# RMSNorm with SiLU on one core: all transfers in turns on one queue

## The chip, the core and the metric

The kernel runs on one core of a Trainium2 chip. The core has a matrix engine (PE), a vector engine (DVE), a scalar engine (ACT), GpSimd (POOL) and SyncE (SP), each with an instruction stream of its own that it works through in order. Data move between device memory (HBM) and the core's own memory (SBUF, 128 partitions) by 16 DMA engines, to which instructions on ACT and SP hand transfers; the page calls the queue that ACT feeds q10 and the one that SP feeds q1. The metric is the device time of one execution in microseconds (us). Lower is better.

## The reference

```python
def setup_inputs():
    batch, seq_len, hidden = 8, 1024, 2048
    return {
        "x": np.random.randn(batch, seq_len, hidden).astype(np.float32),
        "gamma": np.random.randn(hidden).astype(np.float32),
        "eps": np.float32(1e-5),
    }

def reference(x, gamma, eps):
    rms = np.sqrt(np.mean(x ** 2, axis=-1, keepdims=True) + eps)
    out = gamma * x / rms
    return (out * (1 / (1 + np.exp(-out)))).astype(np.float32)
```

There are 8192 rows of 2048 float32 values. Each row is divided by its root mean square, multiplied by gamma and passed through SiLU. Input and output are 67.1 MB each.

## The kernel before

The rows are cut into 16 blocks of 512 rows (4 MB). In a block each of the 128 partitions holds four whole rows that are neighbours in memory, so one partition's share is a run of 32 KB. Six tiles `xt` (BUFS = 6) hold blocks in SBUF, and all work is done in place.

For one block: the squares of each row are summed, some rows on ACT (`squares_scalar`, line 65) and the rest on DVE (`squares_vector`, line 73). `share(b)` on line 78 says how many of the four rows ACT takes: one for the even blocks 4 to 12, two otherwise. ACT then takes the root of the four sums (`root`, line 82), DVE inverts it (`invert`, line 87) and multiplies each row by its own factor and by gamma (`multiply`, line 92). ACT applies SiLU to two rows at a time (`silu`, line 98), and the block is stored (line 102). Root and SiLU use different function tables, so ACT loads a table when it goes from one to the other; squares need no load of their own. The last block is multiplied by gamma alone on DVE (line 155), and ACT applies the row factors as the scale of SiLU (line 157).

Loads are issued on ACT's queue (line 54): blocks 0 and 1 first, blocks 2 to 5 after ACT has waited for gamma (line 116), and each later block b+3 after the first square of block b+1 (lines 67 to 69, 129), when the store that frees its tile has landed. Stores are issued on SP's queue, each when its block's SiLU is done.

Gamma comes in first on SP's queue, as one row of 8 KB on one partition (line 110). PE spreads it over all partitions by matrix products with a column of ones (line 113), and DVE copies the result to `g` (line 115).

The order on ACT and DVE is written out by hand (lines 128 to 149). For each block b the loop places the multiply and SiLU of b among the squares and root of b+1: in the middle (b from 3 to 13) the squares and root of b+1 come ahead of multiply and SiLU of b; at the start and the end the multiply comes first, and SiLU stands between the scalar squares and the root.

Of the kernel before, what the change touches and what calls it, by code (L numbers as in the profile page):

```python
# [1 line left out]

# [4 lines left out]

ACT = mybir.ActivationFunctionType
ALU = mybir.AluOpType


@with_exitstack
def kernel(
    ctx: ExitStack,
    tc: tile.TileContext,
    x: bass.AP,
    gamma: bass.AP,
    eps: bass.AP,
    out: bass.AP,
):  # L20

    nc = tc.nc
    P = nc.NUM_PARTITIONS
    f32 = mybir.dt.float32
    x2 = x.flatten_outer_dims()
    o2 = out.flatten_outer_dims()  # L30
    n, d = x2.shape
    J = 4
    BUFS = 6
    nblk = n // (P * J)
    xb = x2.rearrange("(b p j) d -> b p (j d)", p=P, j=J)
    ob = o2.rearrange("(b p j) d -> b p (j d)", p=P, j=J)

    singles = ctx.enter_context(tc.tile_pool(name="singles", bufs=1))
    pool = ctx.enter_context(tc.tile_pool(name="pool", bufs=BUFS))
    small = ctx.enter_context(tc.tile_pool(name="small", bufs=2))  # L40
    psum = ctx.enter_context(tc.tile_pool(name="psum", bufs=1, space=bass.MemoryType.PSUM))

    Q = 4
    w = d // Q
    g = singles.tile([P, d], f32)
    eps_t = singles.tile([P, 1], f32)
    ones = singles.tile([P, P], f32)
    junk_a = psum.tile([P, d], f32, name="junk_a")
    junk_v = psum.tile([P, d], f32, name="junk_v")
    blocks, sss, rmss, rstds = {}, {}, {}, {}  # L50

    def load(b):
        xt = pool.tile([P, J * d], f32, name="xt")
        nc.scalar.dma_start(out=xt, in_=xb[b])  # L54
        blocks[b] = xt

    def row(b, j):
        return blocks[b][:, j * d:(j + 1) * d]

    def squares_scalar(b, loads=()):  # L60


        sss[b] = small.tile([P, J], f32, name="ss")
        for j in range(share(b)):
            nc.scalar.activation(out=junk_a, in_=row(b, j), func=ACT.Square,  # L65
                                 accum_out=sss[b][:, j:j + 1])
            if j == 0:
                for s in loads:
                    load(s)

    def squares_vector(b):
        for j in range(share(b), J):
            nc.vector.tensor_tensor_reduce(  # L73
                out=junk_v, in0=row(b, j), in1=row(b, j), scale=1.0, scalar=0.0,
                op0=ALU.mult, op1=ALU.add, accum_out=sss[b][:, j:j + 1])

    def share(b):
        return 1 if 4 <= b <= 12 and b % 2 == 0 else 2

    def root(b):  # L80
        rms = small.tile([P, J], f32, name="rms")
        nc.scalar.activation(out=rms, in_=sss.pop(b), func=ACT.Sqrt, scale=1.0 / d, bias=eps_t)  # L82
        rmss[b] = rms

    def invert(b):
        rstd = small.tile([P, J], f32, name="rstd")
        nc.vector.reciprocal(out=rstd, in_=rmss.pop(b))  # L87
        rstds[b] = rstd

    def multiply(b):  # L90
        for j in range(J):
            nc.vector.scalar_tensor_tensor(out=row(b, j), in0=row(b, j), scalar=rstds[b][:, j:j + 1],  # L92
                                           in1=g, op0=ALU.mult, op1=ALU.mult)

    def silu(b):
        for h in range(0, J, 2):
            cols = slice(h * d, (h + 2) * d)
            nc.scalar.activation(out=blocks[b][:, cols], in_=blocks[b][:, cols], func=ACT.Silu)  # L98
        store(b)

    def store(b):
        nc.sync.dma_start(out=ob[b], in_=blocks[b])

    with tc.manual_schedule():

        load(0)
        nc.vector.memset(ones, 1.0)  # L107
        nc.vector.memset(eps_t, float(eps))
        nc.scalar.activation(out=junk_a[:, 0:1], in_=ones[:, 0:1], func=ACT.Square)  # L109
        nc.sync.dma_start(out=g[0:1, :], in_=bass.AP(tensor=gamma.tensor, offset=gamma.offset, ap=[[d, 1], [1, d]]))  # L110
        for c in range(Q):
            cols = slice(c * w, (c + 1) * w)
            nc.tensor.matmul(junk_v[:, cols], ones[0:1, :], g[0:1, cols], start=True, stop=True)  # L113
        load(1)
        nc.vector.tensor_copy(out=g, in_=junk_v)  # L115
        nc.scalar.copy(out=junk_a[:, 0:1], in_=junk_v[:, d - 1:d])  # L116
        for b in range(2, BUFS):
            load(b)

        last = nblk - 1
        SOON = 3
        squares_scalar(0)
        squares_vector(0)
        root(0)
        invert(0)
        for b in range(last):
            loads = [b + 3] if BUFS <= b + 3 < nblk else []
            if b < SOON:  # L130
                multiply(b)
                squares_scalar(b + 1, loads)
                silu(b)
                squares_vector(b + 1)
                root(b + 1)
            elif b < last - 1:
                squares_scalar(b + 1, loads)
                squares_vector(b + 1)
                root(b + 1)
                multiply(b)  # L140
                silu(b)
            else:
                multiply(b)
                squares_scalar(b + 1)
                silu(b)
                squares_vector(b + 1)
                root(b + 1)
            if b + 1 < last:
                invert(b + 1)


        for j in range(J):
            if j == J // 2:
                invert(last)
            nc.vector.tensor_mul(out=row(last, j), in0=row(last, j), in1=g)  # L155
        for j in range(J):
            nc.scalar.activation(out=row(last, j), in_=row(last, j), func=ACT.Silu,  # L157
                                 scale=rstds[last][:, j:j + 1])
        store(last)


# [1 line left out]
_INS = ['x', 'gamma', 'eps']  # L163
_OUTS = [((8, 1024, 2048), 'float32')]

_NUMBERS = {'eps': 9.999999747378752e-06}


# [26 lines left out]
```

## Time and profile before

| | |
|---|---|
| time, median of 3 runs | 316.97 us (316.77 to 317.25) |
| span of the profiled execution | 315.1 us |
| DVE busy | 235.3 us (75%) |
| ACT busy | 213.9 us (68%) |
| PE busy | 7.2 us (2%) |
| DMA packets | 4613, 134.24 MB, mean 426 GB/s over the span |
| loads | 16, 4096 KB each, median 38.7 us from issue to landing |
| stores | 16, 4096 KB each, median 29.0 us from issue to landing |
| DVE's longest wait by line | 42.2 us for loads, ahead of line 73 |

The span runs from the first to the last instruction that the profiler recorded; 1.8 us of the runs' median lie around it. Busy time is time in which an engine computes; issuing a transfer is not counted. The profile's parts used below are the queue table (packets, MB, share of 16 engines' span), the chain of waits (what ended last, followed back), the timeline (start and length in us, engine, line, operation, and in brackets the idle time before it and what ended it), and the table by stretches (for each stretch of the span its length, the busy time and the number of instructions of each engine, the granted clock, the share of the DMA engines' time that its packets took, and GB/s). The packet records beneath the queue table hold the start, length and size of every packet.

### The profile page before, as it was taken

The page shows a single profiled execution, that of the slowest core. Times are in us where ns is not written, and L with a number is a line of the kernel's source. Part 1 is how long each engine was busy: PE and PEld are TensorE (multiplying, and loading weights), DVE is VectorE, ACT ScalarE, POOL GpSimd, SP SyncE. Part 2 cuts the span into 40 slices and gives each one's busy share as a digit, 9 for nine tenths or more (in the row PEclk, how much of TensorE's full clock was granted, in tenths as well). Part 3 has the DMA queues.
Part 4 walks back from the last instruction along what each step waited for, and adds up shares of the span by engine and source line. Part 5 has one row for each costly group of instructions (what it writes and reads, how often), then busy time and mean ns, then how long its engine had stood idle before and what let it go on. Part 6 is the DMA issues. An engine that isn't in the chain of part 4 may idle for free.

```text
span 315.1 us, 439 instructions
## 1 busy us (share of the span) xinstructions
PE 7.2 (2%) x8; PEld 2.5 (1%) x8; DVE 235.3 (75%) x157; ACT 213.9 (68%) x137; POOL 0.2 (0%) x4
## 2 busy tenths in 40 slices
PE   6200000000000000000000000000000000000000
PEld 2000000000000000000000000000000000000000
DVE  0679697979895695957969489593995939999600
ACT  1269998972799258682687827877278768779910
POOL 0000000000000000000000000000000000000000
DMA  8999999999999999999999999999999999999997
GB/s 334 412 453 416 383 458 408 462 403 462 403 459 408 454 412 458 408 462 403 462 403 462 408 458 408 458 408 458 416 449 416 449 416 449 428 437 428 437 428 308
DMA packets 4613, 134.24 MB, mean 426 GB/s; under 512 B 514, under 2 KB 514, under 8 KB 514
## 3 DMA queue, kind: packets, MB, share of 16 engines
q10 hardware_dynamic: 2304, 67.11, 49.8%
q1 hardware_dynamic: 2306, 67.12, 49.3%
q14 instruction: 3, 0.02, 0.0%
HBM read 67.12 MB, written 67.11 MB: 426 GB/s over the span
## 4 chain that ended last, share of the span: by engine, by line
DMA 68%; DVE 14%; ACT 11%; issue 1%; ACTq 1%; DVEq 0%
DMA xt<-in_x_dram 68%; DVE xt L92 9%; DVE junk_v L73 5%; ACT xt L98 4%; ACT junk_a L65 3%; ACT xt L157 2%; ACT L82 1%; ACTq L190 1%; ACT L157 0%; ACT L98 0%; ACT rms L82 0%; DVE ss L73 0%; ACTq L54 0%; DVE rstd L87 0%; ACT L109 0%
## 5 line engine op out<-in xcount | busy, mean ns | idle before, releaser
L92 DVE SCALAR_TENSOR_TENSOR xt<-xt,rstd,g 128x2048 f32<-128x2048 f32 x60 | 137.0, 2346 | 0.1
L98 ACT ACTIVATE xt<-xt 128x4096 f32<-128x4096 f32 x30 | 108.3, 3615 | 27.4 <-DVE xt L92 27.4
L73 DVE CUSTOM_DVE_ANT_0 junk_v<-xt 128x2048 f32<-128x2048 f32 x37 | 85.1, 2299 | 42.9 <-DMA xt<-in_x_dram 42.2
L65 ACT ACTIVATE junk_a<-xt 128x2048 f32<-128x2048 f32 x27 | 50.7, 1876 | 16.1 <-DMA xt<-in_x_dram 14.0
L82 ACT ACT_TABLE_LOAD x15 | 19.2, 1283 | 26.6 <-DVE ss L73 26.5
L98 ACT ACT_TABLE_LOAD x14 | 18.0, 1283 | 0.2
L115 DVE COPY g<-junk_v 128x2048 f32<-128x2048 f32 x1 | 2.3, 2292 | 9.0 <-PE junk_v L113 9.0
L87 DVE RECIPROCAL rstd<-rms 128x4 f32<-128x4 f32 x16 | 2.7, 172 | 8.4 <-ACT rms L82 8.4
L155 DVE TENSOR_TENSOR xt<-xt,g 128x2048 f32<-128x2048 f32 x4 | 8.9, 2277 | 0.0
L82 ACT ACTIVATE rms<-ss,eps_t 128x4 f32<-128x4 f32 x16 | 4.8, 297 | 5.7 <-DVE ss L73 5.5
L157 ACT ACTIVATE xt<-xt,rstd 128x2048 f32<-128x2048 f32 x4 | 7.7, 1991 | 0.0
L113 PE MATMUL junk_v<-g,ones 1*128 1x512 f32 x8 | 7.2, 1072 | 2.8 <-DMA g<-in_gamma_dram 2.8
L116 ACT COPY junk_a<-junk_v 128x1 f32<-128x1 f32 x1 | 0.1, 144 | 9.8 <-DVE g L115 9.8
L73 DVE DVE_READ_ACCUMULATOR2_ANT ss<- 128x1 f32 x37 | 5.2, 141 | 0.0
L65 ACT ACTIVATION_READ_ACCUMULATOR junk_a<-xt 128x1 f32 x27 | 5.0, 186 | 0.0
L113 PEld LDWEIGHTS junk_v<-g,ones 1*128 1x128 f32 x8 | 2.5, 325 | 5.9 <-issue 5.9
L109 ACT ACT_TABLE_LOAD x1 | 1.3, 1283 | 1.1 <-PEq L176 1.1
L157 ACT ACT_TABLE_LOAD x1 | 1.3, 1283 | 0.0
L107 DVE MEMSET ones<- 128x128 f32 x1 | 0.2, 165 | 0.8 <-PEq L176 0.8
L109 ACT ACTIVATE junk_a<-ones 128x1 f32<-128x1 f32 x1 | 0.2, 174 | 0.0
L176 POOL MEMSET const-bfloat16-1.0<- 128x1 bf16 x1 | 0.1, 103 | 0.0
L176 POOL MEMSET const-uint8-127<- 128x1 uint8 x1 | 0.1, 102 | 0.0
(3 smaller groups left out, 0.3 us busy)
## 6 DMA issues: line engine op xcount, KB each, us to landing
xt<-in_x_dram ACTq DMA_DIRECT2D x16, 4096.0 KB, 38.7
out_dram<-xt SPq DMA_DIRECT2D x16, 4096.0 KB, 29.0
g<-in_gamma_dram SPq DMA_DIRECT2D x1, 8.0 KB
```

What stands on the lines that cost most here:

```text
L65: nc.scalar.activation(out=junk_a, in_=row(b, j), func=ACT.Square, accum_out=sss[b][:, j:j + 1])
L73: nc.vector.tensor_tensor_reduce(out=junk_v, in0=row(b, j), in1=row(b, j), scale=1.0, scalar=0.0, op0=ALU.mult, op1=ALU.add, accum_out=sss ...
L82: nc.scalar.activation(out=rms, in_=sss.pop(b), func=ACT.Sqrt, scale=1.0 / d, bias=eps_t)
L87: nc.vector.reciprocal(out=rstd, in_=rmss.pop(b))
L92: nc.vector.scalar_tensor_tensor(out=row(b, j), in0=row(b, j), scalar=rstds[b][:, j:j + 1], in1=g, op0=ALU.mult, op1=ALU.mult)
L98: nc.scalar.activation(out=blocks[b][:, cols], in_=blocks[b][:, cols], func=ACT.Silu)
L109: nc.scalar.activation(out=junk_a[:, 0:1], in_=ones[:, 0:1], func=ACT.Square)
L113: nc.tensor.matmul(junk_v[:, cols], ones[0:1, :], g[0:1, cols], start=True, stop=True)
L115: nc.vector.tensor_copy(out=g, in_=junk_v)
L155: nc.vector.tensor_mul(out=row(last, j), in0=row(last, j), in1=g)
L157: nc.scalar.activation(out=row(last, j), in_=row(last, j), func=ACT.Silu, scale=rstds[last][:, j:j + 1])
L190: with _tile.TileContext(nc) as tc:
```

## The change

All transfers go to SP's queue, in an order fixed ahead of time (`TURNS`): loads of blocks 0 to 5, stores 0 to 4, loads 6 to 10, stores 5 to 9, loads 11 to 15, stores 10 to 15. A transfer is issued when it is next in this order; `issue(done)` is called after each SiLU and hands on everything up to the first store whose block isn't done. SP waits for each transfer's data or for its free slot before it goes on to the next.

The six tiles become one tile of six slots; block b lies in slot b mod 6. Six pairs of neighbouring blocks, (2,3), (4,5), (7,8), (9,10), (12,13) and (14,15), are laid out in memory together: a partition holds eight neighbouring rows, four in each of two adjacent slots. All six pairs are loaded as one transfer of 8 MB with runs of 64 KB, and two of them, (7,8) and (12,13), are also stored so. The other stores move one block.

Gamma is issued behind block 0, as four pieces of 2 KB on partitions 0, 32, 64 and 96; each of PE's four products reads its own piece. The copy to `g` comes after block 0's squares on DVE, which write their unused output to `g`.

ACT takes two rows of squares in every block (`SA = 2`). The loop has three orders: in `AHEAD` the squares and root of b+1 come before multiply and SiLU of b; in `LATE` they come after both; otherwise the multiply comes first and SiLU stands between the scalar squares and the root.

```diff
-    BUFS = 6
+    SLOTS = 6
     nblk = n // (P * J)
-    xb = x2.rearrange("(b p j) d -> b p (j d)", p=P, j=J)
-    ob = o2.rearrange("(b p j) d -> b p (j d)", p=P, j=J)
+    last = nblk - 1
+    PAIRS = ((2, 3), (4, 5), (7, 8), (9, 10), (12, 13), (14, 15))
+    half = {b: (pair[0], k) for pair in PAIRS for k, b in enumerate(pair)}
+    TURNS = (
+        ("load", ((0, 0), (1, 1), (2, 3), (4, 5))),
+        ("store", ((0, 0), (1, 1), (2, 2), (3, 3), (4, 4))),
+        ("load", ((6, 6), (7, 8), (9, 10))),
+        ("store", ((5, 5), (6, 6), (7, 8), (9, 9))),
+        ("load", ((11, 11), (12, 13), (14, 15))),
+        ("store", ((10, 10), (11, 11), (12, 13), (14, 14), (15, 15))),
+    )
+    AHEAD = (1, 2, 3, 7, 9, 12)
+    LATE = (5, 6, 8, 10, 11, 13)
+    def dram(flat, b, e):
+        rows = P * J
+        if b in half:
+            a, k = half[b]
+            run = flat[a * rows:(a + 2) * rows, :].rearrange("(p j) d -> p (j d)", j=2 * J)
+            return run if e > b else run[:, k * J * d:(k + 1) * J * d]
+        return flat[b * rows:(b + 1) * rows, :].rearrange("(p j) d -> p (j d)", j=J)
...
     singles = ctx.enter_context(tc.tile_pool(name="singles", bufs=1))
-    pool = ctx.enter_context(tc.tile_pool(name="pool", bufs=BUFS))
     small = ctx.enter_context(tc.tile_pool(name="small", bufs=2))
     psum = ctx.enter_context(tc.tile_pool(name="psum", bufs=1, space=bass.MemoryType.PSUM))
 
...
     w = d // Q
+    xt = singles.tile([P, SLOTS * J * d], f32, name="xt")
     g = singles.tile([P, d], f32)
+    g4 = singles.tile([P, w], f32)
...
-    blocks, sss, rmss, rstds = {}, {}, {}, {}
...
-    def load(b):
-        xt = pool.tile([P, J * d], f32, name="xt")
-        nc.scalar.dma_start(out=xt, in_=xb[b])
-        blocks[b] = xt
...
+    sss, rmss, rstds = {}, {}, {}
...
+    def rows(b, j, k):
+        at = (b % SLOTS) * J + j
+        return xt[:, at * d:(at + k) * d]
+    def load(b, e):
+        nc.sync.dma_start(out=rows(b, 0, (e - b + 1) * J), in_=dram(x2, b, e))
+    def store(b, e):
+        nc.sync.dma_start(out=dram(o2, b, e), in_=rows(b, 0, (e - b + 1) * J))
+    SA = 2
...
+    def squares_scalar(b):
         sss[b] = small.tile([P, J], f32, name="ss")
-        for j in range(share(b)):
-            nc.scalar.activation(out=junk_a, in_=row(b, j), func=ACT.Square,
+        for j in range(SA):
+            nc.scalar.activation(out=junk_a, in_=rows(b, j, 1), func=ACT.Square,
                                  accum_out=sss[b][:, j:j + 1])
-            if j == 0:
-                for s in loads:
-                    load(s)
...
+    def squares_vector(b, junk=None):
+        for j in range(SA, J):
             nc.vector.tensor_tensor_reduce(
-                out=junk_v, in0=row(b, j), in1=row(b, j), scale=1.0, scalar=0.0,
-                op0=ALU.mult, op1=ALU.add, accum_out=sss[b][:, j:j + 1])
-    def share(b):
-        return 1 if 4 <= b <= 12 and b % 2 == 0 else 2
+                out=junk_v if junk is None else junk, in0=rows(b, j, 1), in1=rows(b, j, 1),
+                scale=1.0, scalar=0.0, op0=ALU.mult, op1=ALU.add, accum_out=sss[b][:, j:j + 1])
 
...
+    queue = [(kind, b, e) for kind, moves in TURNS for b, e in moves]
+    def issue(done):
+        while queue and (queue[0][0] == "load" or queue[0][2] <= done):
+            kind, b, e = queue.pop(0)
+            (load if kind == "load" else store)(b, e)
 
     def silu(b):
         for h in range(0, J, 2):
-            cols = slice(h * d, (h + 2) * d)
-            nc.scalar.activation(out=blocks[b][:, cols], in_=blocks[b][:, cols], func=ACT.Silu)
-        store(b)
-    def store(b):
-        nc.sync.dma_start(out=ob[b], in_=blocks[b])
+            nc.scalar.activation(out=rows(b, h, 2), in_=rows(b, h, 2), func=ACT.Silu)
+        issue(b)
...
     with tc.manual_schedule():
-        load(0)
+        load(*queue.pop(0)[1:])
+        nc.sync.dma_start(out=g4[0:P:P // Q, :],
+                          in_=bass.AP(tensor=gamma.tensor, offset=gamma.offset, ap=[[w, Q], [1, w]]))
+        issue(-1)
         nc.vector.memset(ones, 1.0)
         nc.vector.memset(eps_t, float(eps))
         nc.scalar.activation(out=junk_a[:, 0:1], in_=ones[:, 0:1], func=ACT.Square)
-        nc.sync.dma_start(out=g[0:1, :], in_=bass.AP(tensor=gamma.tensor, offset=gamma.offset, ap=[[d, 1], [1, d]]))
         for c in range(Q):
             cols = slice(c * w, (c + 1) * w)
-            nc.tensor.matmul(junk_v[:, cols], ones[0:1, :], g[0:1, cols], start=True, stop=True)
-        load(1)
+            k = slice(c * (P // Q), c * (P // Q) + 1)
+            nc.tensor.matmul(junk_v[:, cols], ones[k, :], g4[k, :], start=True, stop=True)
+        squares_scalar(0)
+        squares_vector(0, junk=g)
         nc.vector.tensor_copy(out=g, in_=junk_v)
-        nc.scalar.copy(out=junk_a[:, 0:1], in_=junk_v[:, d - 1:d])
-        for b in range(2, BUFS):
-            load(b)
-        last = nblk - 1
-        SOON = 3
-        squares_scalar(0)
-        squares_vector(0)
         root(0)
         invert(0)
         for b in range(last):
-            loads = [b + 3] if BUFS <= b + 3 < nblk else []
-            if b < SOON:
-                multiply(b)
-                squares_scalar(b + 1, loads)
-                silu(b)
-                squares_vector(b + 1)
-                root(b + 1)
-            elif b < last - 1:
-                squares_scalar(b + 1, loads)
+            if b in AHEAD:
+                squares_scalar(b + 1)
                 squares_vector(b + 1)
                 root(b + 1)
                 multiply(b)
                 silu(b)
+            elif b in LATE:
+                multiply(b)
+                silu(b)
+                squares_scalar(b + 1)
+                squares_vector(b + 1)
+                root(b + 1)
             else:
                 multiply(b)
                 squares_scalar(b + 1)
...
             if b + 1 < last:
                 invert(b + 1)
 
...
-        store(last)
+        issue(last)
```

## The prediction

> **What bounds the kernel now.** I read the busy rows and the queue table first. DVE is busy for 75% and ACT for 68% of the span, DMA for nearly all of it: the two queues' packets fill 49.8% and 49.3% of sixteen engines' time, and no slice between the first and the last is under nine tenths.
>
> ```profile
> DMA  8999999999999999999999999999999999999997
> ...
> q10 hardware_dynamic: 2304, 67.11, 49.8%
> q1 hardware_dynamic: 2306, 67.12, 49.3%
> ```
>
> The chain of waits, in order of time, then says what one block costs. In the middle it consists of DMA pieces alone; in each of them two blocks come in and two go out.
>
> ```profile
> 104.80 38.98 DMA xt<-in_x_dram
> 143.78 0.02 issue
> 143.80 0.01 ACT junk_a L65
> 143.81 38.65 DMA xt<-in_x_dram
> 182.46 0.02 issue
> 182.49 0.01 ACT junk_a L65
> 182.50 38.67 DMA xt<-in_x_dram
> ```
>
> ACT's release moves from 143.80 to 182.49: 38.69 for four blocks, 9.67 to 9.68 us for each 4 MB. The packet records behind the DMA table give the same: 32 KB in 1.21 us on each of 16 engines, eight such packets to a block, whether loads run alone, stores alone or both. So the floor is 32 x 9.68 = 309.8 us, and only about 5 us of the span are not transfer at full rate. These I look for in the table by stretches and in the timeline.
>
> ```profile
> 35.00:36.20 1.20, 0.00 (x0) 0.00 (x0) 0.00 (x0) 1.18 (x2) 0.00 (x0) 1.00 1.05 437
> 36.20:38.50 2.30, 0.00 (x0) 0.00 (x0) 1.67 (x2) 2.29 (x4) 0.00 (x0) 1.00 1.38 442
> 38.50:50.00 11.50, 0.00 (x0) 0.00 (x0) 11.47 (x7) 10.68 (x7) 0.00 (x0) 1.00 0.95 410
> ```
>
> The last two columns are DMA share (of the packets that start in the stretch) and GB/s. From 36.2 to 38.5 the share is 1.38: 31 packets took 1.64 us each instead of 1.21, 13.3 us over 16 engines, 0.83 us each. This is 1 us after the first store was issued (35.18); those packets are loads, all of queue q10. No later store does it on all engines.
>
> ```profile
> 0.73 0.38 ACTq L54 DMA_DIRECT2D xt<-in_x_dram  x1
> ...
> 12.38 1.81 ACTq L54 DMA_DIRECT2D xt<-in_x_dram  x4
> 13.08 2.30 DVE L73 CUSTOM_DVE_ANT_0 junk_v<-xt 128x2048 f32<-128x2048 f32 x1 [0.82 <-DMA xt<-in_x_dram]
> ...
> 35.18 53.31 SPq L102 DMA_DIRECT2D out_dram<-xt  x4
> ```
>
> Block 0 is issued at 0.73 into empty queues and lands at 12.97 (DVE starts some 0.11 after a landing; at 104.80 and 104.91 ACT and DVE show it). A block's last packet ends 0.35 before its landing, so an empty queue costs 12.97 - 0.35 - 0.73 - 9.68 = 2.2 us. From 12.97, 31 more blocks would land by 313.1; the last lands near 314.2, and the span ends at 315.15. So 1.2 us are lost on the way, 0.8 to 1.0 of them at the first store.
>
> **The change, part by part.** The sum is made against the span of 315.15; the median of the runs, 316.97, is 1.82 more, and I add that again.
>
> *One queue.* Bytes and engines stay. Rows of loads alone and stores alone run at the same rate as the mixture, so order by itself wins and loses nothing. What can go is the loss at the first store, if it is the price of a queue's first large use; that one engine which q1 had used for gamma lost only 0.5 there speaks for it. It stays if it belongs to the first store. Bounds 0 and 1.2 gained; I take **1.0**. The 16 load issues of 0.33 us leave ACT; there they lay beside DMA.
>
> *64 KB runs.* Eight transfers of pairs (six loads, two stores) have 8 packets per engine instead of 16, if a run stays one packet. That is 64 packets fewer per engine. The trace has no such packet; a 4-byte completion packet takes 0.009 us, so the fixed share is 0 to 0.009, 0 to 0.6 us in all. I take **0.2**. A sentence that the sum doesn't need: the Trainium skill (DMA: Bandwidth & Descriptors, Why small descriptors are slow) puts some 3 cycles on each packet; with the 850 MHz of its bandwidth section my estimate is 64 x 3.5 ns = 0.23.
>
> *Gamma behind block 0.* Its 2 KB packets cost the queue under 0.08 us: **0.05**. It now lands near 13 instead of 2.8; eight matmuls (7.16 us) and the copy (2.29) end near 22.5, and block 0's multiply starts there instead of at 20.18. That is hidden: block 1's multiply now waits in DVE's order behind block 2's squares, thus for the pair (2, 3), which lands at 12.97 + 3 x 9.68 = 42.0.
>
> *Share of squares, order.* ACT now takes two rows of every block (32 squares instead of 27). With both table loads one block costs ACT 6.94 (squares at 88.04 to SiLU at 94.98) + 7.13 (28.03 to 35.17) = 14.07 us, DVE about 14. A block needs 19.4 of DMA, so throughput is covered. But one queue is in order: **a late store now holds up everything behind it**, and the loads after it (block 6 behind store 4, block 11 behind store 9) cannot cover. So each store must be issued before the queue runs dry, and I lay out the three closest.
>
> Store 4: 42.0 landing, DVE starts 42.1, squares 4.61 (85.39 to 90.00), multiply 1 9.13, last SiLU half 3.62: block 1 done 59.5. Then ACT is the chain: blocks 2 and 3 at 14.07 each, 87.6; block 4, whose SiLU stands behind block 5's squares, 3.94 + 7.12: 98.7, issue 98.75. The queue holds ten blocks ahead of it, landed at 12.97 + 9 x 9.68 = 100.1, last packet 0.35 earlier: dry at 99.65 (pairs allowed for). In hand: 0.9 us.
>
> Store 9, counted from the landing t of (7, 8): block 7's squares and root until t+6.6, DVE then block 8's squares (4.6) and multiply 7 (9.13) until 20.5, multiply 8 until 29.9, block 8 done 33.5; ACT's squares of block 9 and its root until 39.2; block 10's squares, multiply 9 until 53.2; SiLU ends 56.8. Ahead in the queue: loads 9-10, stores 5, 6, 7-8, six blocks: dry at t - 0.35 + 58.1 = t+57.7. Again 0.9 in hand.
>
> Store 15, from the landing of (12, 13): block 13 done at 33.5, root 14 39.2, multiply 14 48.6, squares and two gamma products 57.8, four SiLU rows 7.7: 65.6, against 67.4. In hand 1.8. Stores 3, 7-8, 12-13, 14 have 2.3 to 5.5, and no load waits for a store that hasn't long landed.
>
> *What an issue needs before the queue is dry.* This is not in the trace but at its start. Lower bound: first packet of block 0 at 1.77 in the packet records, 1.04 after the issue. Upper: the 2.2 above, which holds first use as well. Four issues in a row take 1.81 us, so writing one transfer's packets to all engines takes about 0.45; the last engine gets them near 1.04 + 0.45. I take **1.5**. Cost: (1.5 - 0.9) at store 4 and again at store 9, nothing at 15: **1.2 us**. Bounds: 0.3 (at 1.04) and 1.3 + 1.3 + 0.4 = 3.0 (at 2.2).
>
> Sum: 315.15 - 1.0 - 0.2 + 0.05 + 1.2 = 315.2, plus 1.82: **317.0 us**, no change that can be told (a measurement of this kernel tells 0.2%, 0.63 us). What the queue regains, two late stores spend.
>
> **Rivals.**
>
> *No gap.* If the 0.9 in hand is enough, nothing is given back: 315.15 - 1.2 = 313.95, time 315.8. For it: the instruction itself is 0.38 of the 1.04, and later issues may start faster than the first. Against: 1.04 is already over 0.9, and engines do not end together (block ends in the records spread by 0.6), so the first engine is dry sooner. This is what a rule of the Trainium skill gives: the same page (Latency and other measured facts) has a first byte from these queues after about 0.6 us; the trace's first packet is 0.66 after the issue row's end and agrees if that is the zero, not if its start is.
>
> *Full price for an empty queue (slower).* Place: stores 4, 9 and 15 at a queue that has just run dry; price 2.2 less what is in hand, 3.0 in all; it decides against the change from a need of about 1.55 us up. 315.15 - 1.2 + 0.05 + 3.0 = 317.0, time 318.8. For it: the only empty start in the trace cost this. Against: that start also was the first use.
>
> *The loss at the first store stays.* 315.15 - 0.2 + 0.05 + 1.2 = 316.2, time 318.0. For it: it came with the first write to the output. Against: the stalled packets were loads, 1 us after the issue, before the store's first packet (39.6).
>
> *Not what it says.* All six slots are one tile; if waits went by tile, load, work and store of a block would follow one another, 16 x (9.7 + 14 + 9.7) = 530 us. Against: before, SiLU works on one half of a tile (79.99) while DVE multiplies in the other (75.35 to 84.48). 64 KB runs cut in two would cost only the 0.2.
>
> **Chances.** Forecast 0.40 (316.3 to 317.8 with its sizes off by a little: of this 0.06 is faster, 0.27 the same, 0.07 slower). No gap 0.27, faster. Full price 0.13, slower. Loss stays 0.17, of which 0.03 within 0.2%. Anything else 0.03, slower. Faster 0.33, same 0.30, slower 0.37. Range 315.5 to 318.6: low end the no-gap case with the bound for longer runs, high end nearly the full price.
>
> **What would show it.** One queue row in the table and 64 fewer data packets per engine and the end of the first-store stall (DMA share 1.0 a few us after the turn at 61). Stores 4 and 9 issued under 1 us before store 3 and pair 7-8 end, and a dip of DMA near 100 and 197 us, each some 0.6 us per engine; none at 304. Block 0's multiply at 22.5 with nothing after it late. Dips of over 1.2, or a third, mean the full price; none means no gap. The forecast is wrong if ACT's 14.07 per block is not kept, or if changes of direction within one queue cost time of their own.

## The result and the profile after

The changed kernel takes 320.13 us (median of 4 runs, 318.45 to 321.43), the kernel before 316.88 us beside it (316.77 to 317.25): a ratio of 1.0099, with a 95% interval of 1.0083 to 1.0115. It is 1.0% slower. The forecast was 317.0 us, and its range ended at 318.6.

The head of the page and the queue table of the changed kernel:

```profile
span 318.2 us, 419 instructions
...
DMA packets 3466, 134.24 MB, mean 422 GB/s; under 512 B 388, under 2 KB 388, under 8 KB 392
...
q1 hardware_dynamic: 3464, 134.23, 98.7%
```

The span is 318.2 against 315.1 before, and 1.8 us lie around it in the profiled run of 319.94. One queue now carries all, with 1147 packets fewer (1024 of them data, 64 per engine, as forecast), and the engines count as nearly always busy. So the 3 us are not a visible hole. They show when landings are compared. In the timeline of the changed kernel, VectorE's rows that a landing releases (start, length, engine, line, operation, and in brackets the idle time before):

```profile
42.10 2.30 DVE L93 CUSTOM_DVE_ANT_0 junk_v<-xt 128x2048 f32<-128x2048 f32 x1 [5.17 <-DMA xt<-in_x_dram]
120.77 2.30 DVE L93 CUSTOM_DVE_ANT_0 junk_v<-xt 128x2048 f32<-128x2048 f32 x1 [11.39 <-DMA xt<-in_x_dram]
140.12 2.30 DVE L93 CUSTOM_DVE_ANT_0 junk_v<-xt 128x2048 f32<-128x2048 f32 x1 [3.55 <-DMA xt<-in_x_dram]
218.87 2.30 DVE L93 CUSTOM_DVE_ANT_0 junk_v<-xt 128x2048 f32<-128x2048 f32 x1 [16.93 <-DMA xt<-in_x_dram]
238.21 2.30 DVE L93 CUSTOM_DVE_ANT_0 junk_v<-xt 128x2048 f32<-128x2048 f32 x1 [3.54 <-DMA xt<-in_x_dram]
```

From 120.77 to 140.12 the pair (7, 8) comes in: 19.35 us for two blocks, the full rate. From 42.10 to 120.77 and from 140.12 to 218.87 the queue moves eight blocks each, which at 9.68 take 77.44. They took 78.67 and 78.75. Both stretches hold two changes of direction (loads to stores, stores to loads); the stretch between them holds none.

What one change costs is read from the packet records: for each of the 16 engines, the time from the start of the last transfer before the change to its first packet after it, less 1.21 us for every 32 KB. I call this the loss at a change.

| change in the changed kernel | about (us) | mean of 16 engines | worst engine |
|---|---|---|---|
| loads to store 0 | 59 | 0.79 | 1.15 |
| store 4 to load 6 | 108.5 | 0.15 | 0.69 |
| loads (9, 10) to store 5 | 156 | 0.81 | 1.36 |
| store 9 to load 11 | 206 | 0.27 | 0.81 |
| loads (14, 15) to store 10 | 254 | 0.89 | 1.74 |

The third row in the DMA view, for the 2.1 us from 155.5, in which just the last packet of the loads starts on each engine (the queue row gives packets, MB and the time they took as a share of 16 engines in that window):

```profile
DMA packets 16, 1.05 MB, mean 499 GB/s; under 512 B 0, under 2 KB 0, under 8 KB 0
...
q1 hardware_dynamic: 16, 1.05, 155.3%
```

155.3% of 2.1 us, shared out over one packet on each engine, is 3.26 us for each packet, where such a packet otherwise takes 2.42. The loss is a lengthened packet, not an idle engine, and it hits the load ahead of the store.

The two stores for which the prediction feared a gap, 4 and 9, in SyncE's timeline:

```profile
98.40 0.33 SPq L81 DMA_DIRECT2D out_dram<-xt  x1
...
196.35 0.33 SPq L81 DMA_DIRECT2D out_dram<-xt  x1
```

By the records, the first engine would have run dry 1.6 us after the issue of store 4 and the last one 2.5 us after; 1.3 and 2.8 us for store 9. At store 4 one engine stood idle for 0.3 us; no other engine waited at either.

### The profile page after: what moved, and what is told of

Read it like the earlier page. It is cut to its first block, busy times and chain, and to the rows that moved or that the text cites. A ratio compares the mean times of both kernels' runs of the same rounds, so it can differ in the third digit from the quotient of the medians.

```text
span 318.2 us, 419 instructions
## 1 busy us (share of the span) xinstructions
PE 2.1 (1%) x8; PEld 0.5 (0%) x8; DVE 223.9 (70%) x147; ACT 215.5 (68%) x140; POOL 0.2 (0%) x4
## 4 chain that ended last, share of the span: by engine, by line
DMA 46%; DVE 25%; ACT 18%; issue 4%; DVEq 1%; SPq 1%; ACTq 1%
DMA xt<-in_x_dram 37%; DVE xt L109 16%; ACT xt L123 10%; DMA out_dram<-xt 8%; DVE junk_v L93 8%; ACT junk_a L88 3%; ACT L99 2%; ACT xt L171 2%; ACT L123 1%; DVEq L204 1%; DVE xt L169 1%; ACTq L204 1%; ACT rms L99 0%; SPq L78 0%; DVE ss L93 0%
## 5 line engine op out<-in xcount | busy, mean ns | idle before, releaser
L93 DVE CUSTOM_DVE_ANT_0 junk_v<-xt 128x2048 f32<-128x2048 f32 x30 | 68.8, 2294 | 41.1 <-DMA xt<-in_x_dram 40.6
L88 ACT ACTIVATE junk_a<-xt 128x2048 f32<-128x2048 f32 x32 | 60.0, 1875 | 41.0 <-DMA xt<-in_x_dram 40.5
L93 DVE CUSTOM_DVE_ANT_0 g<-xt 128x2048 f32<-128x2048 f32 x2 | 4.6, 2293 | 12.0 <-DMA xt<-in_x_dram 12.0
L88 ACT ACTIVATION_READ_ACCUMULATOR junk_a<-xt 128x1 f32 x32 | 6.0, 186 | 0.0
L93 DVE DVE_READ_ACCUMULATOR2_ANT ss<- 128x1 f32 x32 | 4.4, 137 | 0.0
L137 PE MATMUL junk_v<-g,ones 1*128 1x512 f32 x8 | 2.1, 1132 | 13.0 <-DMA g<-in_gamma_dram 13.0
L137 PEld LDWEIGHTS junk_v<-g,ones 1*128 1x128 f32 x8 | 0.5, 305 | 13.0 <-issue 13.0
## 6 DMA issues: line engine op xcount, KB each, us to landing
out_dram<-xt SPq DMA_DIRECT2D x12, 4096.0 KB, 22.5
```

The costliest lines, as they stand in the source:

```text
L88: nc.scalar.activation(out=junk_a, in_=rows(b, j, 1), func=ACT.Square, accum_out=sss[b][:, j:j + 1])
L93: nc.vector.tensor_tensor_reduce(out=junk_v if junk is None else junk, in0=rows(b, j, 1), in1=rows(b, j, 1), scale=1.0, scalar=0.0, op0=AL ...
L137: nc.tensor.matmul(junk_v[:, cols], ones[k, :], g4[k, :], start=True, stop=True)
```

## Experiments

Three theories came first; the expectations name them by letters. By A every change of direction in one queue costs some 0.8 us. By B the runs of 64 KB do it. By C a change to stores costs after a long stretch of loads alone. Kernels whose names begin with m only copy; their expectations say so.

**Runs of 32 KB, same turns, same order on the engines**

```diff
-    PAIRS = ((2, 3), (4, 5), (7, 8), (9, 10), (12, 13), (14, 15))
+    PAIRS = ()
...
-        ("load", ((0, 0), (1, 1), (2, 3), (4, 5))),
+        ("load", ((0, 0), (1, 1), (2, 2), (3, 3), (4, 4), (5, 5))),
```

> The changed kernel without pairs: every transfer is one block with 32 KB runs, same turns, same orders on ACT and DVE. Theory A (each change from loads to stores within one queue costs some 0.8 us per engine): the three stalls near 58, 156 and 254 us stay, time 320 to 321. Theory B (the last 64 KB load packet ahead of a 32 KB store is what is slow): the stalls go, time 315.8 to 317. Theory C (the first store after a phase of loads alone costs it, in whatever queue): as A, 320 to 321.

Measured: 318.74 us, ratio 1.0056 (1.0041 to 1.0071). Losses at the five changes: 0.61, 0.01, 0.05, 0.42, 0.87. Most of the slowdown is there without any long run, so B is out as the main cause. But the third change costs 0.05, with five loads ahead of it as at the fifth, which costs 0.87. This speaks against A and C, and it pointed to what differs between the two. Single transfers land sooner, so that store 4 was issued at 93.4, 6.4 us before the queue ran dry. Store 9 came at 195.59, only 1.1 ahead.

**Stores on ACT's queue**

```diff
-        nc.sync.dma_start(out=dram(o2, b, e), in_=rows(b, 0, (e - b + 1) * J))
+        nc.scalar.dma_start(out=dram(o2, b, e), in_=rows(b, 0, (e - b + 1) * J))
```

> The changed kernel with its stores issued on ACT's queue, right after each SiLU; loads stay on SP's queue in their order, pairs stay. Loads and stores now mix as they become ready. Theory A: no change of direction within a queue is left; one stall of about 0.9 us at the first store as in the kernel before, time 316 to 317. Theory B: stalls stay wherever a 64 KB load packet is followed by a store, time 318 or more. Theory C: only the first store follows a phase of loads alone, so 316 to 317 as A.

Measured: 321.82 us, ratio 1.016 (1.0141 to 1.0179). It is a miss. There is one stall on all engines, at the first store (36 us, 0.8 per engine), as before the change. Then loads and stores share the engines, the loads of 14 and 15 come late, and so do the last two stores: the engines stand idle for about 2 us at 273 and 3.1 at 305. The row of the table by stretches for 304 to 309 of this kernel (the last two columns are DMA share and GB/s) shows the second hole:

```profile
304.00:309.00 5.00, 0.00 (x0) 0.00 (x0) 0.81 (x1) 4.14 (x3) 0.00 (x0) 1.00 0.25 105
```

One stall alone is what A and C expected and B did not; their 316 to 317 us were missed because of the holes. It does not tell A from C.

**Copy alone, turns of several lengths on one queue**

```python
for move in "L0 L1 L2 L3 L4 L5 S0 S1 L6 S2 L7 S3 L8 S4 S5 S6 L9 L10 L11 S7 S8 L12 L13 S9 S10 S11 S12 L14 L15 S13 S14 S15".split():
    (load if move[0] == "L" else store)(int(move[1:]))
```

> No computation: x is copied to the output block by block through the six slots, all on SP's queue, 32 KB runs. Loads come in runs of 6, 1, 1, 1, 3, 2 and 2 blocks, each followed by one or more stores. Theory A: each of the seven changes from loads to stores shows the last load packets longer by some 0.8 us per engine, some 5.6 us in all, span near 319. Theory B: none does, span near 314. Theory C: only after long runs, clearly after 6 blocks (58 us without a store), less or nothing after 1 block (10 us).

Measured: 320.1 us. The first change to stores costs 0.96 (mean of 16 engines); those after one load 0.01, 0.11 and 0.14; after two 0.16 and 0.22; after three 0.10. A is out, since seven changes cost little; B is out again, as there is no 64 KB run. C still stood. Something else appeared: from the third change to stores on, three engines paid 0.4 to 0.8 at each and a fourth 0.1 to 0.65, and the four ended 2 to 4 us after the other twelve. The span of 318.3 lies near the 319 of A, but these four make it, not seven costly changes.

**Copy alone, loads on SyncE's queue, stores on ACT's, in three phases**

```python
for move in "L0 L1 L2 L3 L4 L5 S3 S0 S1 S2 S4 S5 L6 L7 L8 L9 L10 L11 S9 S6 S7 S8 S10 S11 L12 L13 L14 L15 S14 S12 S13 S15".split():
```

> No computation: x is copied to the output block by block, loads on SP's queue and stores on ACT's, 32 KB runs, in three phases; in each the first store is issued while loads are still running and after a time with loads alone, and the next phase's first load waits for the last store, so it is issued into empty queues. Theory A: long load packets 1 us after the first store of the kernel alone, none in phases two and three. Theory C: load packets longer by 0.8 us per engine 1 us after the first store of each of the three phases. Beside that it measures what a load into an empty queue costs when it is not the first: the forecast took 1.5 us from issue (bounds 1.04 and 2.2) beyond 9.68 per block.

Measured: 323.66 us. The first store of each phase, given to a store queue that had run empty, lengthened the packets of loads in flight by 0.80, 0.96 and 0.87 per engine. So the loss at the first store is no price of first use: it came back in each phase. What brings it back is not separated here. The store queue had run empty, but the engines, too, had stood idle for 1.9 us each in the mean before the loads of phases two and three, as at the start of a program. A load given to an empty queue, and not the first, ended 2.36 and 2.23 us later than its 9.68 of transfer, by its slowest engine. That is the prediction's 2.2 without first use.

**Copy alone, phases of one to six loads and as many stores**

```python
PHASES = ((6, None), (1, None), (2, None), (3, None), (4, None), (5, None), (6, None), (1, None), (3, None), (5, None), (2, None), (4, None), (6, None), (4, None), (2, None), (5, None), (3, None), (1, None))
```

> No computation: blocks are copied to the output many times over, all on SP's queue; phases of n loads and then n stores, n in the order 6 1 2 3 4 5, 6 1 3 5 2 4, 6 4 2 5 3 1, 126 transfers. Read is the lengthening of the last load packets ahead of each first store, mean over the engines. Theory A (each change of direction in a queue): 0.8 us for every n. Theory C (time without stores): some 0.9 for n = 6 (58 us), 0.1 for n up to 3 (29 us), a step or slope between; n = 4 and 5 tell where.

Measured: 1238.72 us for 126 transfers. The first change costs 0.88. Later ones after two to six loads, where no phase of a single load stands just ahead, cost 0.00 to 0.14. C is out: six loads in a row cost 0.03 and 0.06, except the first time. Only phases of a single load stand out, where the store must wait for its own load to land and the queue runs dry: 1.5 and 1.6 at the store, then 0.8 to 0.9 at the next change to loads and 0.8 to 1.0 at the next change to stores. (The third such phase ends the run; its store cost 4.1, waiting for an engine that was 3.6 us behind.) **A queue that ran dry went on costing at the changes after it**: this is theory F, that a transfer issued too late is paid for at the next changes of direction.

**Copy alone, phases of six, with small transfers between**

```python
PHASES = ((6, None), (6, 'inside'), (6, 'out'), (6, None), (6, 'inside'), (6, 'out'), (6, None), (6, 'inside'), (6, 'out'))
```

Here 'inside' is a transfer of 128 x 128 values within SBUF in the middle of the loads, 'out' one of that size to the output.

> No computation: nine phases of six loads and six stores on SP's queue; after the third load of a phase comes, in turn, nothing, a small transfer within SBUF (512 bytes a partition), or a small store of that size to the output. Theory C1 (what matters is that the engines' path from SBUF has rested): both kinds of small transfer cut the 0.9 us at the first store to 0.1 to 0.3. Theory C2 (that writes to HBM have rested): only the small store does. Theory A: neither changes it, and the small transfer itself costs another 0.8.

Measured: 1056.35 us. The first change costs 0.90; the two later phases without any small transfer, 58 us without a store, cost 0.03 and 0.1. There was nothing left for the small transfers to save; each cost 0.2 itself.

**Turns of two on one queue, in the full kernel**

```diff
-        ("load", ((0, 0), (1, 1), (2, 3), (4, 5))),
-        ("store", ((0, 0), (1, 1), (2, 2), (3, 3), (4, 4))),
...
+        ("load", ((0, 0), (1, 1), (2, 2), (3, 3))),
+        ("store", ((0, 0),)),
+        ("load", ((4, 4), (5, 5))),
+        ("store", ((1, 1), (2, 2))),
...
-    AHEAD = (1, 2, 3, 7, 9, 12)
-    LATE = (5, 6, 8, 10, 11, 13)
+    AHEAD = (2, 10, 11, 14)
+    LATE = (6, 7, 8, 9)
```

> The computation and gamma as in the changed kernel, all transfers on SP's queue with 32 KB runs, but in short turns: loads 0 to 3, store 0, loads 4 and 5, then two stores and two loads by turns, and the orders on ACT and DVE chosen for it so that every store is issued 6 us or more before its queue is dry. Theory A (each change of direction costs 0.8): 13 changes, half of them to stores, some 5 us: 320 to 321. Theory C (time without stores): one stall, at store 0: 315.5 to 316.8. A mixed case, C and a lag that a few engines gather at each change as in the copy with short runs: 317 to 319.

Measured: 319.78 us, ratio 1.0093 (1.0076 to 1.011). Every store is issued 6.7 us or more ahead, but for the last two (3.6 and 4.8), which have no change behind them. The first change costs 0.86 and the other twelve at most 0.13 each, by the mean of the engines. But two engines pay 0.3 to 1.1 at nearly every change to stores from the third on. They end at 315.8 and 316.5, the other fourteen between 313.1 and 314.0. So it is the mixed case of the expectation, 0.8 us above its range. The mean and the slowest engine tell different stories here, and the time is the slowest engine's.

**Theory F, first in the full kernel: only the order of work on ACT and DVE changed, so that stores 4 and 9 come earlier**

```diff
-    AHEAD = (1, 2, 3, 7, 9, 12)
-    LATE = (5, 6, 8, 10, 11, 13)
+    AHEAD = (0, 2, 3, 7, 9, 12, 14)
+    LATE = (4, 5, 6, 10, 11)
```

> The changed kernel itself, pairs and turns unchanged, with other orders on ACT and DVE, so that stores 4 and 9 are issued 3 to 4 us before the queue is dry instead of 1.3 to 1.6. Theory F: the costs at the changes near 108, 156, 206 and 254 us (2.1 us by mean over the engines) go, the first one stays; time 317 to 318.3 against 320.1. Theory A or C: 320 as before.

Measured: 317.31 us (11 runs), ratio to the kernel before 1.001 (1.0001 to 1.002). Same transfers in the same turns, same runs, same queue, and 2.8 us less than the changed kernel; the slowest of these 11 runs (318.27) is still under the fastest of the changed kernel's four (318.45). In this kernel's timeline of SyncE, the loads behind store 4 are handed over at 95.57, right after it, instead of 98.79, and store 9 is issued 2.04 us sooner than the changed kernel's:

```profile
95.57 16.09 SPq L78 DMA_DIRECT2D xt<-in_x_dram  x3
...
194.31 0.33 SPq L81 DMA_DIRECT2D out_dram<-xt  x1
```

Store 4 now has 5.1 us in hand at its first engine and store 9 has 2.7. The new order brings other stores nearer to dry: (7, 8), (12, 13) and 14 have 2.4 to 2.6, where they had 4.8 to 5.5. Losses at the five changes: 1.10, 0.03, -0.02, 0.07, 0.20. The same DMA view as above, from 155.5 to 157.6, for this kernel:

```profile
DMA packets 16, 1.05 MB, mean 499 GB/s; under 512 B 0, under 2 KB 0, under 8 KB 0
...
q1 hardware_dynamic: 16, 1.05, 115.8%
```

115.8% of 2.1 us is 2.43 us for each packet: the 3.26 are gone. And its landings:

```profile
140.32 2.30 DVE L93 CUSTOM_DVE_ANT_0 junk_v<-xt 128x2048 f32<-128x2048 f32 x1 [3.55 <-DMA xt<-in_x_dram]
217.72 2.30 DVE L93 CUSTOM_DVE_ANT_0 junk_v<-xt 128x2048 f32<-128x2048 f32 x1 [17.82 <-DMA xt<-in_x_dram]
237.06 2.30 DVE L93 CUSTOM_DVE_ANT_0 junk_v<-xt 128x2048 f32<-128x2048 f32 x1 [3.54 <-DMA xt<-in_x_dram]
```

140.32 to 217.72 is 77.40, the full rate for eight blocks, where the changed kernel took 78.75. From the last of these rows to the end of the span it is 79.1 against 79.9. These two differences, 1.35 and 0.8, less 0.2 lost earlier, are the 2.0 us between the two spans (316.2 and 318.2). The profiled run of this kernel, 317.98, is one of its slower ones, so the traces lie closer together than the medians.

**The same with runs of 32 KB and single transfers**

```diff
-    PAIRS = ((2, 3), (4, 5), (7, 8), (9, 10), (12, 13), (14, 15))
+    PAIRS = ()
...
-    AHEAD = (1, 2, 3, 7, 9, 12)
-    LATE = (5, 6, 8, 10, 11, 13)
+    AHEAD = (0, 1, 2, 3, 6, 7, 8, 12, 13)
+    LATE = (4, 5, 9, 10)
```

> The kernel of e1_runs32 (32 KB runs, same turns, all on SP's queue) with other orders on ACT and DVE, chosen so that every store is issued 7 us or more before its queue is dry; transfers and their order are unchanged. Theory F (a transfer issued less than some 1.5 to 2 us ahead of the dry point costs nothing there, but the engines pay 0.8 to 1.2 us at the next changes of direction): only the first change (near 61 us) costs, the 0.42 and 0.87 behind store 9 go; time 316.6 to 317.8 against 318.7. Theory A or C (changes of direction or time without stores by themselves): no different from e1_runs32, 318.7 or above.

Measured: 317.32 us (11 runs), ratio 1.0015 (1.0006 to 1.0024). All stores have 7 us or more in hand. The first change costs 0.66, the other four 0.00 to 0.06. The engines end at 313.41 in the mean (313.44 before the change), but one ends at 314.6, where the last one before the change ended at 313.96. That one engine is all of the 0.65 us between the two profiled spans (315.80 and 315.15); the medians differ by 0.4.

**Copy alone, the fifth store of each phase held back by work on ACT**

```python
WAITS = ((0, 0), (9, 800), (10, 1400), (9, 3150), (10, 2550), (10, 200), (10, 3130), (10, 800), (10, 1970), (0, 0))
def hold(c, full, part):
    for k in range(full):
        nc.scalar.copy(out=slot(c)[:, 0:4096], in_=slot(c)[:, 0:4096])
    if part:
        nc.scalar.copy(out=slot(c)[:, 0:part], in_=slot(c)[:, 0:part])
```

> No computation of the reference: blocks are copied on SP's queue in ten phases of five loads and five stores; in all but the first and last phase a chain of copies on ACT holds back the fifth store, so that it is issued, in this order, about 6, 2, 4, 1, 3, 0.5, 2.5 and 1.5 us before the queue runs dry. Read is the cost at the two changes of direction behind it. Theory F: under 0.2 us by mean where the store was 3 us or more ahead, 0.8 to 2 us where it was 1.5 or less ahead. Theory A: the same at every change. Theory C: the same behind every phase of five loads.

Measured, in us; the middle columns are the mean of 16 engines in excess of the full rate:

| issue ahead of dry (first / last engine) | at the store | next change, to loads | next, to stores |
|---|---|---|---|
| not held back | 0 | 0 | 0.02 |
| 3.9 / 4.7 | 0 | 0 | 0.05 |
| 2.4 / 2.8 | 0 | 0 | 0.03 |
| 1.1 / 1.7 | 0 | 0.38 | 1.01 |
| 0.6 / 1.2 | 0.07 | 0.86 | 0.79 |
| -0.4 / 0.6 | 0.83 | 0.88 | 0.64 |
| -0.6 / 0.1 | 1.10 | 0.90 | 0.45 |
| -1.0 / -0.5 | 1.57 | 0.86 | 0.75 |
| -2.5 / -0.8 | 3.00 | 0.85 | 0.95 |

The DMA view of this kernel from 392.0 to 392.7, where only the held-back store's last packet starts on each engine (row 2.4 / 2.8):

```profile
q1 hardware_dynamic: 16, 0.52, 173.3%
```

The same view from 789.5 to 789.9 (row 0.6 / 1.2):

```profile
q1 hardware_dynamic: 16, 0.52, 492.6%
```

173.3% of 0.7 us is 1.21 for each packet, the normal length. 492.6% of 0.4 is 1.97. In the second no engine had stood idle for more than a moment, 0.07 in the mean, and yet the last packet ahead of the next loads is 0.76 longer. **That is F**: with 2.4 us or more in hand a late store is free; with 1.7 or less it leaves hardly a gap and costs 1.4 to 1.7 us at the next two changes; really late, it costs both. No row of this copy lies between 1.7 and 2.4. By engine, in the row 1.1 / 1.7, the seven with under 1.3 us in hand lost 0.5 to 0.9 at the next change to loads and the other nine 0.2 or less, but at the change after it all 16 lost 0.5 to 1.5.

**A small transfer on the queue ahead of the first store, without and with the change**

```diff
+    spare = singles.tile([P, P], f32)
...
+        nc.sync.dma_start(out=spare, in_=ones)
```

In the first kernel it stands behind load 0 of the 32 KB version with early stores, in the second behind gamma in the kernel before the change.

> The kernel of e4_early32 with one small transfer from SBUF to SBUF (512 bytes a partition) on SP's queue behind load 0. It asks whether the one cost that is left, 0.7 to 1.1 us at the first change to stores, is paid by a small transfer out of SBUF early on. If it is: 316.4 to 316.9 and no dip at 61 us. If the cost belongs to the first full change whatever went before: 317.3 to 317.5 as e4_early32 or 0.2 more.

> The kernel before with the same small transfer on SP's queue behind gamma. If the loss of 0.8 to 1 us at the first store is the price of that queue's first transfer on all 16 engines, it goes: 315.9 to 316.3. If it is the price of a queue that starts again after it was empty, it stays: 316.8 to 317.1.

Measured: 317.44 us, ratio 1.0015 (1.0006 to 1.0024), for the first; 317.31 us, ratio 1.001 (1.0002 to 1.0019), for the second. Neither gains. The first still loses 0.7 per engine at its first change to stores, and the second still loses 0.88 per engine when its first store comes (0.89 without the small transfer). A small transfer on all 16 engines of the store's queue, long before, does not take the loss away.

No kernel here beat the one before: the two with early stores are 0.1% and 0.15% slower than it.

## Why the prediction was wrong, step by step

**What bounds the kernel** was right: 9.68 us per 4 MB, and a few us lost that are not transfer.

**The compute chain** was right and is not the cause. The chain of waits of the changed kernel, in order of time (start, length, engine, tile and line):

```profile
42.10 2.30 DVE junk_v L93
...
80.31 7.12 ACT xt L123 x2
87.44 1.90 ACT junk_a L88 x2
...
91.36 7.02 ACT xt L123 x2
...
98.79 0.42 SPq L78
99.30 40.80 DMA xt<-in_x_dram
```

Block 3's SiLU begins at 80.31, block 4's behind block 5's squares at 91.36, and the store is out at 98.40; 98.75 was forecast, and blocks 2 and 3 took 13.97 each instead of 14.07. Store 9 came 56.3 after the landing it was counted from (56.8 forecast), store 15 came 65.0 after its own (65.6).

**Gamma** was right in that it cost nothing on the path, but its own times were forecast too long. The four products, in the timeline of the changed kernel, and block 0's multiply:

```profile
13.04 2.09 PE L137 MATMUL junk_v<-g,ones 1*128 1x512 f32 x8 [13.04 <-DMA g<-in_gamma_dram]
...
20.12 9.14 DVE L109 SCALAR_TENSOR_TENSOR xt<-xt,rstd,g 128x2048 f32<-128x2048 f32 x4
```

The products take 2.09 us instead of 7.16, and the multiply starts at 20.12, not at 22.5. Neither is on the path.

**64 KB runs** were right: a run stays one packet of 65,536 bytes. By the records a pair takes 19.32 us on an engine, from start to start, and two single blocks 2 x 9.68 = 19.36; eight transfers saved some 0.3 us in all (0.2 forecast).

**The loss at the first store** failed as a term of -1.0. It did not go with ACT's queue but moved to the first change of direction (0.79 mean, about 0.9 before): -0.1 in place of -1.0. The rival "the loss stays" had this part right. The hint that the prediction had leaned on, one engine that gamma had used and that lost only 0.5, did not bear it: with the small transfer on all 16 engines 0.88 stayed.

**The late stores** are the step that failed in its mechanism. The prediction set a need of 1.5 us against 0.9 in hand, and a price of 0.6 at stores 4 and 9 themselves. There was a little more in hand, 1.6 and 1.3 us at the first engine, since the stores came 0.35 and 0.45 us earlier than forecast and, at store 4, the dry point lay 0.3 later. At the place itself next to nothing was lost. The copy with the held-back store puts the need at the place at some 0.9 us (row -0.4 / 0.6: 0.06 in hand in the mean, 0.83 lost). (The Trainium skill, DMA: Bandwidth & Descriptors, section Latency and other measured facts, has a first byte from these queues after about 0.6 us; of the 0.9, 0.33 are the issue row, so the run agrees with 0.6 behind that row.) By the prediction's own arithmetic that would have been the rival "no gap" at 315.8. The cost came at the changes of direction behind the late stores, which the working had dismissed with "order by itself wins and loses nothing": 0.15 + 0.81 after store 4, 0.27 + 0.89 after store 9, together 2.1 us against 1.2 forecast, at places where the prediction had put nothing. The rows it argued from, loads alone, stores alone and both at the same rate, were all of well-filled queues. Its own last sentence had named such changes as what would make it wrong, without a price in the sum. "Full price", at 318.8, came nearest in time, but its 2.2 us for an empty queue at three places were not seen at any of them, so that this nearness is luck. (The need from which that rival turns the sum, given as about 1.55 us, comes to just under 1.5 by its own terms: 2 x 0.575 makes the 1.15 gained.)

**One engine behind the others** was not in the forecast at all. Before, the 16 engines end at 313.44 in the mean and the last at 313.96. In the changed kernel the mean is 315.25 and the last 316.96, so that one engine adds 1.2 us more than before. The span follows the last engine: in both traces, and in those of the two kernels with early stores, it ends 1.19 us after it. This term does not belong to the late stores, or only in part, for with early stores the last engine still ends 1.3 and 1.2 us after the mean. Its cause stays open.

The sum with the measured sizes: -0.1 (first change) - 0.3 (long runs) + 2.1 (later changes) + 1.2 (slowest engine) = +2.9, against 318.15 - 315.15 = 3.0.

That one queue should be as good as two follows from a rule of the Trainium skill (the same page, section Issuing engines are not separate DMA queues): spreading transfers over issuing engines saves issue time only. The two kernels with early stores agree within 0.1 to 0.15%; the changed kernel, at 1.0%, does not.

## What to carry to other kernels

When transfers are moved to one queue in a fixed order, work out for each how long before the queue runs dry it is issued, and give it 2.5 us or more; here that alone was worth 2.8 of the 3.25 us, by the order of work on engines that were not the bound. A late transfer need not show as a gap: look for lengthened packets at the next changes of direction, and compare landings some blocks apart with the full rate. And look at the slowest of the 16 DMA engines, not at their mean, since a transfer is done when its last engine is.

## What was not expected of the hardware

- A queue that is nearly dry costs later. Why the price of up to 1.0 us per engine falls on the next change, and on the one after it as well, stays open.
- The first change from loads to stores in a program, or the first store on a queue that had stood empty, costs 0.6 to 1.1 us per engine in every kernel here, on one queue or on two. Later changes in a well-filled queue cost 0.00 to 0.22. This may be theory F once more, since in all of them the first load, too, went to an empty queue; no run here sets a store queue's restart apart from engines that stood idle before.
- Single engines keep paying at changes that cost the others nothing (two engines 0.3 to 1.1 each time in the turns of two, four engines 0.1 to 0.8 in the copy in turns), and end up to 4 us late. What marks them out stays open; it was not tried.
- A load into an empty queue costs 2.2 to 2.4 us at its slowest engine, first use or not; a store into a queue just run dry about 0.9.
